# The low half of every weight chunk is split off when the next chunk's split begins

## The chip, the cores and the metric

The kernel runs on one core of a Trainium2 chip. The metric is the device time of one execution in microseconds; the median of several runs of the kernel before is 2160.03 us.

## The reference, cut to what matters

Two transformer blocks are computed in float32 on 512 tokens of width 1024. The first is an S5 state-space mixer beside a sliding-window attention, then a gated FFN; the second is a dilated-window attention, an FFN, an HGRN2 mixer, and an FFN. The bulk is products of a 512 x 1024 activation with weights:

```python
proj = hn @ w_in[l]                                   # mix
h = h + rms_norm(merged @ w_out[l], g_post_mix[l])
gu = hn @ w_gate_up[l]                                # ffn1
ff = (jax.nn.silu(gu[..., :D_FF]) * gu[..., D_FF:]) @ w_down[l]
...
proj = (x @ w_in).reshape(B, S, N_GROUPS, 3, ATTN_HEADS, ATTN_HEAD_DIM)   # attn
return jnp.square(jax.nn.relu(x @ w_up)) @ w_down                         # ffn2_0, ffn2_1
q_raw, f_raw, i_raw = jnp.split(x @ w_in, [H * K, 2 * H * K], axis=-1)    # hgrn
```

## The kernel before, in words

The stages run one after the other: mix, ffn1, attn, ffn2_0, hgrn, ffn2_1. The activations stay in SBUF. All weights are packed beforehand in the order of their use into 328 chunks of 128 x 1024 float32 values, and the class `Stream` feeds them to every stage.

A product in float32 is made of three TensorE passes on reduced-precision operands: each operand is split into a high part, `hi`, and a low part, `lo = value - hi`, and hi·hi, hi·lo and lo·hi are added in PSUM. For weights this split is done in `Stream._split`: SP starts the DMA of a chunk into one of three `wst` buffers (L170), ScalarE (ACT) copies it rounded into `whi` (L183), and VectorE (DVE) subtracts to get `wlo` (L184). There are 6 buffers (`SLOTS`) of `whi` and `wlo`. For activations the split is at L312 and L313 (`xh` on ACT, `xl` on DVE), for the hidden values of the FFN at L469 and L470 (`hh`, `hl`).

Each engine executes its instructions in the order in which the program issues them. `take` hands out the chunks that are used next and first calls `prefetch`, which splits up to `ahead` = 4 chunks further on, at most 5 past the oldest chunk of the same `take`; `more` does the same in the middle of a product. `_split(i)` also starts loads up to chunk i + 2, and such a load has to wait until its `wst` buffer was read by the `hi` and the `lo` of three chunks ago.

In an FFN stage `up` takes one chunk for each 128 rows of hidden values (24 matmuls of 512 columns, L260 to L262), applies the activation function (`hid`: `r`, `h`, `hh`, `hl`, L464 to L470 in ffn2), and `down` takes four chunks at once for the product with w_down (96 matmuls, L370 to L372). `banks` (L357 to L385) sets the order of those 96. A stage begins with `up_first`, which takes four chunks and computes their first 256 columns while the layer norm of the last tokens (L343 to L355: `nm`, `x` L350, `x` L352) is still under way. In mix, the first chunk (u0) is split before everything else by `prefetch(0, 0)`.

Of the kernel before, what the change touches and what calls it, by code (L numbers as in the profile page):

```python
# [26 lines left out]
F32 = mybir.dt.float32  # L27
# [128 lines left out]
class Stream:  # L156
# [3 lines left out]

    def __init__(self, K, labels, dram):
        self.K, self.labels, self.dram = K, labels, dram
        self.loaded, self.split, self.used = 0, 0, 0
        self.st, self.hl = {}, {}

    def _load(self):
        i = self.loaded
        if i < len(self.labels):
            t = self.K.wst.tile([128, CE], F32, name="wst")
            self.K.nc.sync.dma_start(t, self.dram[i])  # L170
            self.st[i] = t
        self.loaded += 1

    def _split(self):
        i = self.split
        K = self.K
        while self.loaded <= i + self.STAGE_AHEAD:
            self._load()
        if i < len(self.labels):
            t = self.st.pop(i)  # L180
            hi = K.wsp.tile([128, CE], FR, name="whi")
            lo = K.wsp.tile([128, CE], FR, name="wlo")
            K.nc.scalar.activation(hi, t, AF.Copy)  # L183
            K.nc.vector.tensor_sub(lo, t, hi.bitcast(F32))  # L184
            self.hl[i] = (hi, lo)
        self.split += 1

    def prefetch(self, upto, oldest):

        while self.split <= min(upto, oldest + self.SLOTS - 1):  # L190
            self._split()
# [5 lines left out]
    def take(self, *labels, ahead=AHEAD):  # L197

        i0, out = self.used, []
        for label in labels:  # L200
            i = self.used
            assert self.labels[i] == label, (self.labels[i], label)
            self.prefetch(i + ahead, i0)
            self.used += 1
            out.append(self.hl.pop(i))
        return out

# [1645 lines left out]
```

## Time and profile before

| what | value |
|---|---|
| median of 3 runs | 2160.03 us (2159.95 to 2162.28) |
| profiled execution | 2164.82 us, its span 2163.0 us |
| mean granted clock of TensorE | 0.982 |
| busy share PE / PEld / DVE / ACT / POOL | 96% / 81% / 56% / 37% / 12% |
| all waits of PE for other engines, added up | about 62 us |
| DVE at `wlo` L184, busy | 436.3 us in 328 instructions |
| ACT at `whi` L183, busy | 331.7 us in 328 instructions |
| weight chunk, from issue of its DMA to landing | 3.8 us (median) |
| spacing of matmuls, read from the timelines | 0.23 us (512 columns), 0.12 us (256 columns), 0.21 us (256 columns at the lower clock) |

PE is TensorE's matmuls and PEld its weight loads, which run beside the matmul before. What PE waits for decides the time; idle time of the other engines costs nothing by itself. In the rows further down, a bracket as [0.33 <-DVE wlo L184] says how long the engine was idle before the row and who released it. Of consecutive DVE rows the next one starts some 0.07 us before the recorded end of the one before.

### The profile page before, as it was taken

Reading aid. Unit: us, or ns where it says so; the run is one execution under the profiler, and the core shown is the slowest. Engines: PE = TensorE matmul, PEld = TensorE weight load, DVE = VectorE, ACT = ScalarE, POOL = GpSimd, SP = SyncE. Lnnn points to the kernel's source line nnn. Section 1 sums busy time; section 2 is a strip of 40 time slices with the busy share of each in tenths; the row PEclk is TensorE's granted clock in tenths of the full one; section 3 lists DMA queues with packets and bytes.
Section 4 is the critical chain, followed back from the end, with each engine's and each line's share of the span. In section 5 each row is a group of like instructions: output and inputs, shape, how many; then the busy total and the mean of one; then the engine's idle time right before and its main releaser. Section 6 shows DMA issues by size and latency. Waiting matters only on the chain.

```text
span 2163.0 us, 30385 instructions
## 1 busy us (share of the span) xinstructions
PE 2083.6 (96%) x12196; PEld 1759.6 (81%) x12196; DVE 1217.7 (56%) x2129; ACT 793.1 (37%) x1470; POOL 269.7 (12%) x325
## 2 busy tenths in 40 slices
PE   6888999999999999999998999999999999999997
PEld 5876788888888888888887888888888878888885
DVE  6876453334366666667766644444565566444444
ACT  5346343222233444443344432223254434222331
POOL 3740100000003212121220100000100001000001
PEclk9979999999999999999999999999999999999998
DMA  3201232223225333333333222232232222222221
GB/s 128 79 23 40 108 117 98 98 78 117 98 68 188 116 113 118 108 98 109 107 115 130 87 89 98 78 108 97 91 106 69 79 78 88 100 85 97 100 96 69
DMA packets 75662, 209.35 MB, mean 97 GB/s; under 512 B 21248, under 2 KB 26016, under 8 KB 75520
## 3 DMA queue, kind: packets, MB, share of 16 engines
q1 hardware_dynamic: 66560, 181.13, 25.0%
q0 software_dynamic: 6816, 19.83, 3.2%
q10 hardware_dynamic: 2144, 6.45, 0.9%
q8 instruction: 96, 1.57, 0.3%
q14 instruction: 46, 0.38, 0.1%
HBM read 186.29 MB, written 4.29 MB: 88 GB/s over the span
## 4 chain that ended last, share of the span: by engine, by line
PE 57%; issue 24%; DVE 3%; POOL 1%; ACT 1%; DMA 1%; POOLq 0%; ACTq 0%; DVEq 0%
PE mm L260 13%; PE mm L261 13%; PE mm L262 13%; PE dn L371 4%; PE dn L370 4%; PE dn L372 4%; PE o L741 1%; PE dn L669 1%; DVE P L648 1%; DVE wlo L184 1%; POOL rv L306 1%; POOL rr L308 1%; PE dn L720 1%; PE dn L718 0%; DMA wst<-in_wstream 0%
## 5 line engine op out<-in xcount | busy, mean ns | idle before, releaser
L260 PE MATMUL mm<-xh,whi 128*128 128x512 f32 (+1 forms) x1488 | 562.7, 378 | 8.4 <-ACT whi L183 5.3
L261 PE MATMUL mm<-xl,whi 128*128 128x512 f32 (+1 forms) x1488 | 558.1, 375 | 2.7 <-DVE xl L313 2.7
L262 PE MATMUL mm<-xh,wlo 128*128 128x512 f32 (+1 forms) x1488 | 557.5, 375 | 0.5 <-DVE wlo L184 0.5
L184 DVE TENSOR_TENSOR wlo<-wst,whi 128x1024 fp32r<-128x1024 f32 x328 | 436.3, 1363 | 167.0 <-ACT whi L183 165.9
L183 ACT ACTIVATE whi<-wst 128x1024 fp32r<-128x1024 f32 x328 | 331.7, 1050 | 353.6 <-PE dn L371 222.0
L260 PEld LDWEIGHTS mm<-xh,whi 128*128 128x128 f32 x1488 | 282.8, 190 | 63.0 <-ACT whi L183 5.6
L261 PEld LDWEIGHTS mm<-xl,whi 128*128 128x128 f32 x1488 | 282.9, 190 | 52.3 <-DVE xl L313 3.8
L262 PEld LDWEIGHTS mm<-xh,wlo 128*128 128x128 f32 x1488 | 282.8, 190 | 51.5 <-DVE wlo L184 0.8
L371 PE MATMUL dn<-whi,hl 128*128 128x512 f32 x688 | 271.5, 395 | 0.0
L370 PE MATMUL dn<-whi,hh 128*128 128x512 f32 x688 | 271.0, 394 | 0.1
L372 PE MATMUL dn<-wlo,hh 128*128 128x512 f32 x688 | 268.5, 390 | 0.0
L260 PE MATMUL mm<-whi,xh 128*128 128x256 f32 x608 | 177.3, 292 | 1.9 <-DVE kT L1197 1.9
L261 PE MATMUL mm<-wlo,xh 128*128 128x256 f32 x608 | 173.3, 285 | 0.0
L262 PE MATMUL mm<-whi,xl 128*128 128x256 f32 x608 | 173.1, 285 | 0.0
L480 DVE SCALAR_TENSOR_TENSOR x<-x,dn 128x512 f32<-128x512 f32 x112 | 75.6, 685 | 169.1 <-PE dn L372 169.1
L306 POOL TENSOR_SCALAR rv<-ss 128x1 f32<-128x1 f32 (+1 forms) x42 | 26.3, 626 | 1041.9 <-ACT junk L348 443.2
L370 PEld LDWEIGHTS dn<-whi,hh 128*128 128x128 f32 x688 | 129.4, 188 | 30.4 <-DVE x L341 0.5
L372 PEld LDWEIGHTS dn<-wlo,hh 128*128 128x128 f32 x688 | 129.3, 188 | 29.3
L371 PEld LDWEIGHTS dn<-whi,hl 128*128 128x128 f32 x688 | 129.5, 188 | 26.7
L260 PEld LDWEIGHTS mm<-whi,xh 128*128 128x128 f32 x608 | 117.8, 194 | 7.3 <-issue 4.6
L261 PEld LDWEIGHTS mm<-wlo,xh 128*128 128x128 f32 x608 | 117.9, 194 | 0.2
L262 PEld LDWEIGHTS mm<-whi,xl 128*128 128x128 f32 x608 | 117.8, 194 | 0.0
(385 smaller groups left out, 2542.9 us busy)
## 6 DMA issues: line engine op xcount, KB each, us to landing
wst<-in_wstream SPq DMA_DIRECT2D x328, 512.0 KB, 3.8
qks<-qkT POOLq DMA_DIRECT2D x96, 128.0 KB, 2.8
v<-gb SPq DMA_DIRECT2D x128, 32.0 KB, 1.8
X<-in_x SPq DMA_DIRECT2D x4, 512.0 KB, 7.7
xn<-in_x POOLq DMA_DIRECT2D x4, 512.0 KB, 4.5
x_d<-x POOLq DMA_DIRECT2D x4, 512.0 KB, 6.7
x<-x_d POOLq DMA_DIRECT2D x4, 512.0 KB, 6.9
out<-x SPq DMA_DIRECT2D x4, 512.0 KB, 2.6
```

The source lines that it names most:

```text
L183: K.nc.scalar.activation(hi, t, AF.Copy)
L184: K.nc.vector.tensor_sub(lo, t, hi.bitcast(F32))
L260: mm(ps, wh, xh, start=first, stop=False, skip_group_check=True)
L261: mm(ps, wh, xl, start=False, stop=False, skip_group_check=True)
L262: mm(ps, wl, xh, start=False, stop=last, skip_group_check=True)
L306: self.nc.gpsimd.tensor_scalar(v[:, :n], ss, scale, eps, op0=OP.mult, op1=OP.add)
L308: self.nc.gpsimd.tensor_tensor(r[:, :n], v[:, :n], self.nhalf[:, :n], op=OP.pow)
L370: mm(p, hT[i][0][:, c], w[i][0][:, n], start=i == 0, stop=False)
L371: mm(p, hT[i][1][:, c], w[i][0][:, n], start=False, stop=False)
L372: mm(p, hT[i][0][:, c], w[i][1][:, n], start=False, stop=i == m - 1)
L480: nc.vector.scalar_tensor_tensor(x, x, ALPHA if first else 1.0, ps, op0=OP.mult, op1=OP.add)
L648: nc.vector.tensor_scalar(s, s, E[:, g, u, h:h + 1], None, op0=OP.mult)
```

## The change

`_split` no longer issues the subtraction directly behind the copy. It notes it in `self.due`, and `low` issues it either when the next chunk's split begins or when `take` hands out the chunk itself.

```diff
@@ __init__
         self.st, self.hl = {}, {}
+        self.due = None
...
     def _split(self):
         i = self.split
         K = self.K
+        self.low()
         while self.loaded <= i + self.STAGE_AHEAD:
             self._load()
...
             K.nc.scalar.activation(hi, t, AF.Copy)
-            K.nc.vector.tensor_sub(lo, t, hi.bitcast(F32))
             self.hl[i] = (hi, lo)
+            self.due = i, lo, t, hi
         self.split += 1
+
+    def low(self, upto=None):
+
+        if self.due and (upto is None or self.due[0] <= upto):
+            _, lo, t, hi = self.due
+            self.due = None
+            self.K.nc.vector.tensor_sub(lo, t, hi.bitcast(F32))
...
             self.prefetch(i + ahead, i0)
             self.used += 1
+            self.low(i)
             out.append(self.hl.pop(i))
```

The order of instructions on PE, ACT, POOL and SP is the same in both kernels; on DVE only the `wlo` rows move. In the rows of the changed kernel line numbers are 10 or 11 higher (L184 is L195, L470 is L480, L352 is L362).

On DVE, in ffn2_0, this is the stretch around the first `down` of the stage. `h` and `hl` belong to the hidden values of four `up` chunks, the `wlo` rows are chunks of this `down` and, in the row marked x2 or x3, also of the next `up`, and the x rows add the output of `down`. Before:

```order
L184 TENSOR_TENSOR wlo<-wst,whi 128x1024
L466 TENSOR_TENSOR h<-r 128x512
L470 TENSOR_TENSOR hl<-h,hh 128x512
L184 TENSOR_TENSOR wlo<-wst,whi 128x1024
L466 TENSOR_TENSOR h<-r 128x512
L470 TENSOR_TENSOR hl<-h,hh 128x512
L184 TENSOR_TENSOR wlo<-wst,whi 128x1024 x2
L480 SCALAR_TENSOR_TENSOR x<-x,dn 128x512 x8
```

In the changed kernel:

```order
L195 TENSOR_TENSOR wlo<-wst,whi 128x1024
L476 TENSOR_TENSOR h<-r 128x512
L480 TENSOR_TENSOR hl<-h,hh 128x512
L195 TENSOR_TENSOR wlo<-wst,whi 128x1024
L476 TENSOR_TENSOR h<-r 128x512
L480 TENSOR_TENSOR hl<-h,hh 128x512
L195 TENSOR_TENSOR wlo<-wst,whi 128x1024 x2
L490 SCALAR_TENSOR_TENSOR x<-x,dn 128x512 x8
```

The single `wlo` ahead of the last `h` and `hl` was the fourth chunk of the `down`; now it is the third, and the fourth is the first of the two behind `hl`.

On DVE, at the start of ffn2_0, `nm`, `x` and `x` are the layer norm of the last 128 tokens and `xl` is the split of the transposed activations. Before:

```order
L184 TENSOR_TENSOR wlo<-wst,whi 128x1024
L345 TENSOR_SCALAR nm<-sums_ln_mix_g_10315 128x1
L350 SCALAR_TENSOR_TENSOR x<-x,nm,gb 128x1024
L352 SCALAR_TENSOR_TENSOR x<-x,rr,gb 128x1024
L184 TENSOR_TENSOR wlo<-wst,whi 128x1024
L313 TENSOR_TENSOR xl<-dn,xh 128x4x128 x4
```

In the changed kernel:

```order
L195 TENSOR_TENSOR wlo<-wst,whi 128x1024
L355 TENSOR_SCALAR nm<-sums_ln_mix_g_10314 128x1
L360 SCALAR_TENSOR_TENSOR x<-x,nm,gb 128x1024
L362 SCALAR_TENSOR_TENSOR x<-x,rr,gb 128x1024
L195 TENSOR_TENSOR wlo<-wst,whi 128x1024 x2
L323 TENSOR_TENSOR xl<-dn,xh 128x4x128 x4
```

The `wlo` of the third chunk of ffn2_0 stood ahead of `nm`; now it stands behind the second `x`, in front of the fourth chunk's.

On DVE, at the start of mix, the X rows scale the input, and `fr` and `fi` are the last of some forty small instructions that prepare the rotation angles. Before:

```order
L892 SCALAR_TENSOR_TENSOR X<-X,rr,gb 128x1024 x2
L184 TENSOR_TENSOR wlo<-wst,whi 128x1024
L313 TENSOR_TENSOR xl<-dn,xh 128x4x128 x2
L892 SCALAR_TENSOR_TENSOR X<-X,rr,gb 128x1024
...
L960 TENSOR_TENSOR fr<-t_0_185,t_1_186 128x16
L961 TENSOR_TENSOR fi<-t_3_188,t_1_186 128x16
L184 TENSOR_TENSOR wlo<-wst,whi 128x1024 x2
L313 TENSOR_TENSOR xl<-dn,xh 128x4x128 x4
```

In the changed kernel:

```order
L902 SCALAR_TENSOR_TENSOR X<-X,rr,gb 128x1024 x2
L323 TENSOR_TENSOR xl<-dn,xh 128x4x128 x2
L902 SCALAR_TENSOR_TENSOR X<-X,rr,gb 128x1024
L323 TENSOR_TENSOR xl<-dn,xh 128x4x128 x2
...
L970 TENSOR_TENSOR fr<-t_0_184,t_1_185 128x16
L971 TENSOR_TENSOR fi<-t_3_187,t_1_185 128x16
L195 TENSOR_TENSOR wlo<-wst,whi 128x1024 x3
L323 TENSOR_TENSOR xl<-dn,xh 128x4x128 x4
```

The first chunk's `wlo` stood third, ahead of the first `xl`; now it is the first of three behind the angles.

## Rows read from the trace of the kernel before

**Rows 1.** The page, part 1: busy us (share of the span) xinstructions of each engine.

```profile
PE 2083.6 (96%) x12196; PEld 1759.6 (81%) x12196; DVE 1217.7 (56%) x2129; ACT 793.1 (37%) x1470; POOL 269.7 (12%) x325
```

**Rows 2.** Waits of the whole span: engine, line, releaser: us in total, times, longest.

```profile
DVE wlo L184 <- ACT whi L183: 165.9, 128, 20.2
```

**Rows 3.** Waits of the DMA-issuing queue of SP, with the same columns.

```profile
SPq L170 <- DVE wlo L184: 1600.2, 283, 77.2
```

**Rows 4.** Line 184: durations (min/median/max ns), first and last start, forms.

```profile
L184 DVE TENSOR_TENSOR wlo<-wst,whi x328: 1209/1221/4197, 11.4 to 2127.5; 128x1024 fp32r<-128x1024 f32 x164
```

**Rows 5.** Timeline near 1772 us: start us, duration us, engine, line, [idle before <-releaser].

```profile
1771.78 0.39 PE L371 MATMUL dn<-whi,ol 128*128 128x512 f32 x1
...
1772.07 0.19 PEld L372 LDWEIGHTS dn<-wlo,oh 128*128 128x128 f32 x1 [0.33 <-DVE wlo L184]
...
1772.40 0.39 PE L370 MATMUL dn<-whi,oh 128*128 128x512 f32 x1
```

**Rows 6.** Timeline of ffn2_0 around its first change from up to down products.

```profile
1290.47 1.23 DVE L184 TENSOR_TENSOR wlo<-wst,whi 128x1024 fp32r<-128x1024 f32 x1 [0.26 <-ACT whi L183]
...
1295.11 0.69 DVE L470 TENSOR_TENSOR hl<-h,hh 128x512 fp32r<-128x512 f32 x1 [0.70 <-ACT hh L469]
...
1296.51 0.19 PEld L372 LDWEIGHTS dn<-wlo,hh 128*128 128x128 f32 x1
```

**Rows 7.** Timeline of the start of mix (0 to 92 us).

```profile
16.25 0.42 PE L262 MATMUL mm<-xh,wlo 128*128 128x256 f32 x1
...
26.84 0.17 DVE L961 TENSOR_TENSOR fi<-t,t 128x16 f32<-128x16 f32 x1
...
27.16 0.58 PE L260 MATMUL mm<-xh,whi 128*128 128x256 f32 x1 [5.32 <-ACT whi L183]
...
32.22 1.04 PE L325 MATMUL dn<-ident,X 128*128 128x128 f32 x8
...
45.40 1.23 DVE L184 TENSOR_TENSOR wlo<-wst,whi 128x1024 fp32r<-128x1024 f32 x1 [3.87 <-ACT whi L183]
...
90.86 0.69 PE L1193 MATMUL mm<-ident,qk 128*128 128x128 f32 x2 [4.59 <-ACT v L1221]
```

**Rows 8.** Timeline of mix, first group of products with w_out.

```profile
217.93 0.40 PE L372 MATMUL dn<-wlo,oh 128*128 128x512 f32 x1
...
218.21 0.75 DVE L1353 SCALAR_TENSOR_TENSOR ol<-sig,m_g_so,oh 128x512 fp32r<-128x512 f32 x1 [0.79 <-ACT oh L1352]
```

**Rows 9.** Timeline of the start of ffn2_0.

```profile
1207.88 1.28 DVE L352 SCALAR_TENSOR_TENSOR x<-x,rr,gb 128x1024 f32<-128x1024 f32 x1 [0.71 <-POOL rr L308]
...
1208.03 0.28 PE L262 MATMUL mm<-xh,wlo 128*128 128x256 f32 x1
```

**Rows 10.** Timeline of the start of hgrn.

```profile
1569.85 0.28 PE L262 MATMUL mm<-xh,wlo 128*128 128x256 f32 x1
...
1572.31 1.22 DVE L184 TENSOR_TENSOR wlo<-wst,whi 128x1024 fp32r<-128x1024 f32 x1
```

**Rows 11.** Timeline of the end of ffn1: two down products back to back.

```profile
616.38 0.69 DVE L1723 TENSOR_TENSOR acc<-acc,dn 128x512 f32<-128x512 f32 x1 [2.06 <-PE dn L372]
...
617.10 0.19 PEld L372 LDWEIGHTS dn<-wlo,hh 128*128 128x128 f32 x1
```

**Rows 12.** Timeline of the end of attn.

```profile
1138.86 0.39 PE L372 MATMUL mm<-wlo,xh 128*128 128x512 f32 x1
...
1140.58 1.90 DVE L776 TENSOR_TENSOR xl<-x,xh 128x512 fp32r<-128x512 f32 x3 [2.45 <-ACT xh L775]
...
1146.01 1.35 PE L669 MATMUL dn<-qkT 64*128 64x128 f32 x7 [4.31 <-DVE ML L637]
```

**Rows 13.** Timeline of the start of ffn1.

```profile
272.89 0.39 PE L260 MATMUL mm<-xh,whi 128*128 128x256 f32 x1 [3.03 <-ACT xh L312]
```

**Rows 14.** Windows: each engine's busy us (instructions), granted TensorE clock, DMA share, GB/s.

```profile
272.80:276.00 3.20, 2.77 (x12) 2.58 (x13) 2.99 (x4) 2.50 (x5) 1.53 (x4) 0.56 0.41 154
...
1146.00:1150.00 4.00, 3.99 (x20) 3.48 (x21) 3.93 (x32) 3.46 (x16) 0.00 (x0) 0.50 0.98 382
```

## The prediction

> **What bounds the kernel now.** I read the busy times first: PE is busy for 96% of the span, DVE for 56% [rows 1]. So the time changes only where PE waits more or less. The table of waits comes next. Before its `wlo`, DVE stands 128 times for the ACT copy that feeds it, 165.9 us in all, and everything behind it on DVE stands too [rows 2]. This is what the change can shorten: the subtraction is issued when its input has long been there. But DVE is not the bound; all that PE waits for, on any engine, is about 62 us in the table ahead. So I went to the timelines and asked of each of the 328 chunks: when does PEld first want its `wlo`, and what stands on DVE in front of it now. What is saved is mostly idle time on an idle engine; what is paid is every place where `wlo` now comes after PEld wants it.
>
> **The change part by part.** Nothing is added or removed: 328 subtractions of 1.22 us (median) stay [rows 4], and PE, ACT, POOL and SP keep their order. What moves is each `wlo` on DVE, past what stands between its own split and the next one.
>
> *The price of a late `wlo`* is in the trace: a weight load waited 0.33 us. The matmul two rows on would have come at 1771.78 + 2 x 0.23 = 1772.24 and came at 1772.40, 0.16 late [rows 5]. A weight load runs ahead of its matmul, so the delay is the lateness less some 0.17 us, and nothing below that.
>
> *Up to down in ffn2.* The fourth `down` chunk's `wlo` ran at 1290.47, far ahead of its use. Now it stands behind `h` and `hl` of the last `up` chunk. `hl` runs from 1295.11 to 1295.80, so `wlo` runs from about 1295.73 to 1296.95, and PEld wants it at 1296.51 [rows 6], with 0.05 us for the signal 0.49 late, which costs 0.32. There are 7 such changes in each of ffn2_0 and ffn2_1: 14 x 0.32 = 4.5 us, between 0 (if `hl` comes half a microsecond earlier) and 14 x 0.49 = 6.9. In ffn1 the same reading leaves 0.2 us to spare; I take nothing.
>
> *Starts of a stage.* The third chunk's `wlo` now stands behind the last norm. In ffn2_0 `x` L352 starts at 1207.88 and takes 1.28; `wlo` would end at 1207.88 + 1.20 + 1.22 = 1210.30. The matmul that needs it came at 1208.03 [rows 9]: 2.25 us late. In hgrn six small instructions are in front as well: `wlo` would start at 1572.31 where another one did before, end at 1573.53, and was needed at 1569.85 [rows 10], 3.7 us. The starts of ffn1 and ffn2_1 read the same way give 2.6 and 2.55. The four together: 11.1 us.
>
> *Two `down` products back to back.* At the end of ffn1 the last chunk's `wlo` now waits for the last addition. That starts at 616.38 and takes 0.69, so `wlo` ends near 616.99 + 1.22 = 618.21, and PEld wants it at 617.10 [rows 11]: 1.1 late, about 1.0 of delay. The ends of ffn2_0 and ffn2_1 repeat it, the last chunks of w_out in hgrn give about 1.2, the first product of attn about 0.65. Together 5.0.
>
> *Mix, w_out.* `wlo` now follows `ol`, which starts at 218.21 and takes 0.75: 218.89 to 220.11. Its matmul came at 217.93 [rows 8]. That is 2.2 at most. DVE no longer stands for the copy earlier in the group, which may bring `ol` up to 1 us forward: 1.2 to 2.2, I take 1.7.
>
> *End of attn.* `wlo` of the fourth chunk of w_out follows three `xl`, 1140.58 to 1142.48, and ends near 1143.65. Its matmul came at 1138.86 [rows 12]: about 4.8 us. But 4.31 us of waiting follow at 1146.01, for the softmax behind the same DVE work. After the stall come 6 matmuls (1.4 us at full pace, 2.7 at half), about 0.9 us of scores and three softmax rows of 0.35: 1147.2 to 1148.5. So PE goes on 1.2 to 2.5 us later than at 1146.01; I take 2.0.
>
> *Start of mix.* The first `wlo` moves past 41 instructions behind the angles (L961 at 26.84). The matmul that needs it came at 16.25 and now comes at about 28.3. The 22 that follow it, some at half pace, take some 4.1 us, transposes 0.8, the next 24 matmuls 24 x 0.12 = 2.9: the transposes that stood at 32.22 come at about 36.1, +3.9. Before, PE idled here anyhow: 5.32 us until 27.16. DVE then stood 3.87 us for a copy at 45.40 [rows 7] and about 2.9 a little later; these end, so DVE is some 3 us ahead where it hands its tables to POOL, and the wait of 4.59 at 90.86 [rows 7] shrinks by that. With 0.5 us for a later small exposure the start of mix is worth -1.5, between -4 and +4.
>
> *What is given back elsewhere.* DVE is free earlier in the tails of the stages. From mix to ffn1 2.1 us of standing for a copy go, and I take 2.25 off PE's waits there, of which the largest is the 3.03 at 272.89 [rows 13]. In the same way hgrn's tail gives 1.25, the other stage ends 1.85, softmax in attn 1.0: -6.3, between -2 and -12.
>
> The sum: 4.5 + 11.1 + 5.0 + 1.7 + 2.0 - 1.5 - 6.3 = +16.5. Some of the 11.1 falls where PE would have waited for the same norm shortly after; I take 1.5 off for it and say **+15**. The profiled execution then goes from 2164.82 to about 2180; it is 4.8 above the median of the runs, which goes from 2160.03 to about **2175**. A measurement of this kernel tells about 0.2% (4.3 us) from no change.
>
> **The clock.** After the wait of 3.03 at 272.89 the granted clock was 0.56 over the next 3.2 us, after the 4.31 at 1146.01 it was 0.50 over 4 us [rows 12 to 14]: near half pace, the lower of the two levels, a loss of some 1.5 to 2 us each. After the 0.33 at 1772.07 matmuls kept 0.23 [rows 5]. So the small stalls cost no more than themselves. Those of 2.25 to 3.7 us at the starts of stages lie near the one that lowered the clock.
>
> The Trainium skill, "TensorE: Matmul & The Clock Gate", section "Why this matters for your kernels", warns that a gap between bursts of matmuls brings the clock back to the lower level, which the two waits above bear out. [...]
>
> **The rivals.** *Larger, some +20 to +25* (chance 0.18). The four starts lose the clock, 4 x 1.75 = +7, on top of 15: 2182. For it speaks [rows 13, 14]; against it that the stalls split a burst instead of following a longer gap. A mechanism in the same direction: SP's loads stand for `wlo` 283 times [rows 3], and each `wst` buffer now comes free one split later; where several splits are bunched the copy could wait for its DMA. Against it: a load lands in 3.8 us and the `up` chunks are used every 5.6.
>
> *No measurable change* (chance 0.12). The starts of stages cost half, 5.5, because norms come earlier with a freer DVE, the start of mix gives 4, the tails 9: 4.5 + 5.5 + 5 + 1.7 + 2 - 4 - 9 = +6, and a small miss elsewhere brings it within 4.3. That needs nearly every bound at its good end.
>
> *Faster* (chance 0.05). One mechanism: in mix, PE waits for DVE and ACT in the chain of tables, scans and rotations, among them the 5.32 and 4.59 of [rows 7]. If DVE's standing behind the copies is what delays that chain, mix gives back much more than 1.5. It decides from 15 + 4.3 + 1.5 = 21 us in mix; the 5.32 can't go, since its copy stands on ACT, and the 4.59 with its loss of clock is worth 6.5. So this is unlikely.
>
> **How the numbers follow.** My forecast, +8 to +20, has 0.65; the larger case 0.18, no change 0.12, faster 0.05. Slower is the first two, 0.83. The range leaves out about one in ten on each side: from +4 (2164) to +24 (2184).
>
> **What the profile of the changed kernel would show.** PE and PEld in `down` wait for `wlo` 14 times by some 0.3 to 0.5 us in ffn2; single waits of 2 to 4 us for `wlo` stand at the starts of ffn1, ffn2_0, hgrn and ffn2_1, about 1 us at three ends of stages, 12 us near 28 us. DVE's 165.9 us of waits for `whi` shrink to a small part. ACT and POOL keep their busy times. The prediction is wrong if PE's waits for `wlo` add up to less than 15 us beside the one at 28, or if PE's waits for other work in mix and the tails shrink by more than 10.

## The result, and the profile after

The changed kernel took 2182.02 us (median of 4 runs, 2179.74 to 2184.02), the kernel before 2160.77 on the same chip. The ratio is 1.0097, with a 95% interval of 1.0082 to 1.0111: 18 to 24 us slower. The prediction said 2175 (2164 to 2184).

The page of the changed kernel, parts 1 and 5, answers to [rows 1]. No engine has noticeably more to do, DVE even less, and yet the span is longer.

```profile
span 2178.0 us, 30330 instructions
...
PE 2082.9 (96%) x12196; PEld 1754.6 (81%) x12196; DVE 1186.1 (54%) x2129; ACT 794.4 (36%) x1470; POOL 267.5 (12%) x325
...
L195 DVE TENSOR_TENSOR wlo<-wst,whi 128x1024 fp32r<-128x1024 f32 x328 | 400.6, 1251 | 110.4 <-ACT whi L185 109.6
```

This is what line 195, the moved subtraction, does now: durations, what DVE idled for in front of it, and who waited for it (us, times).

```profile
L195 DVE TENSOR_TENSOR wlo<-wst,whi x328: 1210/1220/2325, 26.9 to 2142.6; 128x1024 fp32r<-128x1024 f32 x164
...
  ACT whi L185: 109.6, 33
...
  PEld mm L272: 22.7, 8
  PE mm L272: 21.0, 8
  PEld dn L382: 16.8, 22
  PE dn L382: 6.3, 5
  PEld mm L382: 5.1, 1
  PEld mm L271: 5.0, 3
  PE mm L382: 4.7, 1
  PE mm L271: 4.4, 3
```

Both halves of the exchange are here. DVE stood for the copy 33 times instead of 128, but still for 109.6 us of the 165.9 [rows 2]: two thirds of its standing stayed. The longest subtraction fell from 4197 ns [rows 4] to 2325, and all of them together from 436.3 us of work to 400.6. In return PEld, which had waited for `wlo` in hardly any place, waits 34 times and 49.6 us in all. PE's own waits for `wlo` went from 0.5 us to 36.4, all its other waits together from 62.2 to 40.8. The net is 14.5 us, close to the 14.9 us by which the two profiled executions differ.

With both kernels' matmuls laid side by side in program order (PE's order is the same), the difference of the two start times, the lateness, shows where time goes. Five rows of the changed kernel, in the order of the program: two at the start of mix, then a group of w_out, the end of attn and the start of hgrn.

```profile
28.19 0.58 PE L272 MATMUL mm<-xh,wlo 128*128 128x256 f32 x1 [11.76 <-DVE wlo L195]
...
89.83 0.44 PE L1203 MATMUL mm<-ident,qk 128*128 128x128 f32 x2 [0.25 <-ACT v L1231]
...
219.46 0.49 PE L382 MATMUL dn<-wlo,oh 128*128 128x512 f32 x1 [3.13 <-DVE wlo L195]
...
1143.20 0.79 PE L382 MATMUL mm<-wlo,xh 128*128 128x512 f32 x1 [4.68 <-DVE wlo L195]
...
1577.78 0.39 PE L272 MATMUL mm<-xh,wlo 128*128 128x256 f32 x1 [3.04 <-DVE wlo L195]
```

The first matmul of mix that needs a low part came at 16.25 [rows 7] and comes at 28.19. By the row at 89.83, which was at 90.86 with a wait of 4.59 [rows 7], PE is 1.0 us ahead of before: the chain on POOL that it waits for started earlier. At 219.46 it falls 1.5 behind (217.93 in [rows 8]). It is 4.0 behind at the start of attn, gets back to about 0 by its end, and from ffn2_0 on it loses: 3.6 us behind at the start of ffn2_0, 7.9 at the start of hgrn (1569.85 in [rows 10]), 15.1 at the last product. In ffn2 the stall looks like this (DVE, DVE, PEld), to be held against [rows 6]:

```profile
1298.11 0.69 DVE L480 TENSOR_TENSOR hl<-h,hh 128x512 fp32r<-128x512 f32 x1 [0.70 <-ACT hh L479]
...
1298.71 2.35 DVE L195 TENSOR_TENSOR wlo<-wst,whi 128x1024 fp32r<-128x1024 f32 x2
...
1299.98 0.19 PEld L382 LDWEIGHTS dn<-wlo,hh 128*128 128x128 f32 x1 [0.47 <-DVE wlo L195]
```

The two profiled executions differ by 14.9 us (2164.82 and 2179.74), the medians by 21. The profiled execution of before is on the slow side of its runs, the one of after on the fast side of its own; sizes in time below are therefore from the timed runs, and places from the traces.

### The profile page after: what moved, and what is told of

The parts are those of the page before. It is cut to its first block, busy times and chain, and to the rows that moved or that the text cites. A ratio compares the mean times of both kernels' runs of the same rounds, so it can differ in the third digit from the quotient of the medians.

```text
span 2178.0 us, 30330 instructions
## 1 busy us (share of the span) xinstructions
PE 2082.9 (96%) x12196; PEld 1754.6 (81%) x12196; DVE 1186.1 (54%) x2129; ACT 794.4 (36%) x1470; POOL 267.5 (12%) x325
## 3 DMA queue, kind: packets, MB, share of 16 engines
q1 hardware_dynamic: 66560, 181.13, 24.6%
## 5 line engine op out<-in xcount | busy, mean ns | idle before, releaser
L195 DVE TENSOR_TENSOR wlo<-wst,whi 128x1024 fp32r<-128x1024 f32 x328 | 400.6, 1251 | 110.4 <-ACT whi L185 109.6
L476 DVE TENSOR_TENSOR h<-r 128x512 f32<-128x512 f32 x64 | 44.3, 692 | 133.5 <-ACT r L474 133.5
```

Of the source, the lines that this page charges most:

```text
L195: self.K.nc.vector.tensor_sub(lo, t, hi.bitcast(F32))
L476: nc.vector.tensor_mul(h, r, r)
```

## The experiments

All ten kernels split the 328 chunks into those that are deferred as in the change and those whose low part is issued directly behind the copy, as before. Each time is compared with the kernel before, run beside it (medians 2162.04 to 2162.18 us). The edit is two lines in the changed kernel's `_split`, with a set of chunk numbers:

```diff
             self.due = i, lo, t, hi
+            if i not in LATE:
+                self.low()
```

**Only what was waited for is kept early.** All chunks are deferred but 31 of the 34 that PEld waited for; before the change it already waited for the other three.

```diff
+NOW = {0, 9, 17, 24, 85, 89, 163, 169, 170, 179, 187, 195, 203, 211, 219, 227, 229, 233, 234, 237, 261, 265, 266, 275, 283, 291, 299, 307, 315, 323, 325}
...
             self.due = i, lo, t, hi
+            if i in NOW:
+                self.low()
```

> The changed kernel, but for 31 chunks whose low part was waited for in its trace (the first, single ones in mix, attn and hgrn, the second and third at the starts of stages, the last before a product that follows another directly, and the fourth of 14 products in ffn2) the subtraction is issued directly behind the copy again; the other 297 stay deferred. Theory (late low parts cost, a freer DVE gives back): the costs go and the gains stay, by the two traces some 5 us at the start of mix, 3 in the tail of mix, 4 in the softmax of attn, 2 in other tails: 2146 to 2154 us, against 2160.8 before. Rival (deferral itself is harmful, since each load is freed later): within 3 us of before, or slower than it.

2151.49 us, ratio 0.9953 (0.9940 to 0.9965): 8 to 13 us faster than before. Deferral as such does no harm; its price lies in those 31 of 328 chunks. This run also settles what the prediction feared of the loads. ACT's copies do wait longer for their DMA when everything is deferred, but they do so here as well, in a version that is faster than before. These are the waits of before, of the change and of this run, in us, times and longest:

```profile
ACT whi L183 <- DMA wst<-in_wstream: 47.1, 14, 6.5
...
ACT whi L185 <- DMA wst<-in_wstream: 134.5, 35, 6.9
...
ACT whi L188 <- DMA wst<-in_wstream: 135.9, 35, 6.8
```

**The fourth chunk of 14 `down` products.**

```diff
+LATE = {179, 187, 195, 203, 211, 219, 227, 275, 283, 291, 299, 307, 315, 323}
```

> The kernel before with one part of the change: only the fourth chunk of 14 products with w_down in ffn2_0 and ffn2_1 is deferred behind h and hl. Theory (a late low part costs its lateness less what the weight load is ahead): 14 x 0.3 to 0.4 us, +4 to +5.5 us. Rival 1 (hidden): within 1.5 us of before. Rival 2 (every small stall also lowers the clock): over +15 us.

2166.71 us, ratio 1.0022 (1.0012 to 1.0031): +4.8 us (2.6 to 6.7). In its timeline, one of the stalls, and the matmul after it:

```profile
1845.79 0.19 PEld L387 LDWEIGHTS dn<-wlo,hh 128*128 128x128 f32 x1 [0.54 <-DVE wlo L200]
...
1846.13 0.39 PE L385 MATMUL dn<-whi,hh 128*128 128x512 f32 x1
```

A load 0.54 late costs about 0.4, and the matmul spacing behind it stays as before: the granted clock over the next 4 us is 1.00.

**Starts of stages.**

```diff
+LATE = {24, 170, 234, 266}
```

> The kernel before with one part of the change: only the third chunk of ffn1, ffn2_0, hgrn and ffn2_1 is deferred, behind the norm of the last tokens. Theory: four stalls of 1.5 to 3.3 us and some of the clock behind them, +8 to +13 us. Rival (the stalls stand in for waits on the same norm shortly after): less than +4 us.

2167.99 us, ratio 1.0034 (1.0022 to 1.0046): +7.4 us (4.8 to 9.9), just under the +8 to +13 of the theory. Laid beside before, the four chunks lose 0.6, 1.5, 2.8 and 1.7 us at their stalls; in the whole change the same four lose 1.7, 2.2, 3.3 and 2.2. The difference is on DVE. Alone, moving the third chunk's subtraction lets the norm in front of it start about 1 us sooner; in the whole change the second chunk's subtraction has moved into the gap. The rival is out: no wait shortly behind the stalls of ffn1, ffn2_0 and ffn2_1 takes their loss back, and behind hgrn's it is 0.9 us.

**The first chunk.**

```diff
+LATE = {0}
```

> The kernel before with one part of the change: only the very first chunk's low part is deferred, behind the angles. Theory (the early stall is paid, and only the other deferrals in mix win it back): TensorE about 4 us late at 45 us and still some 3 to 4 us late at 91 us, +3 to +5 us. Rival (the idle time that was there before and the chain of tables on GpSimd take it up by themselves): within 1 us of before.

2165.63 us, ratio 1.0018 (1.0009 to 1.0026): +3.9 us (1.9 to 5.6). Its DVE still stands for the two next copies (first two rows). PE, 5.1 us late at the transposes of 32.22, still waits for the same `v` behind POOL's chain, 5.3 us later than at 90.86 in [rows 7]:

```profile
50.55 1.23 DVE L200 TENSOR_TENSOR wlo<-wst,whi 128x1024 fp32r<-128x1024 f32 x1 [3.90 <-ACT whi L188]
56.64 1.23 DVE L200 TENSOR_TENSOR wlo<-wst,whi 128x1024 fp32r<-128x1024 f32 x1 [2.87 <-ACT whi L188]
...
96.11 0.69 PE L1208 MATMUL mm<-ident,qk 128*128 128x128 f32 x2 [4.68 <-ACT v L1236]
```

So the early idle time takes up only a part of the late first chunk; the other deferrals in mix do the rest.

**Mix and attn alone.** Deferred are mix, the first chunks of ffn1 (22 to 33) and attn up to number 159, without five that were waited for.

```diff
+LATE = (set(range(34)) | set(range(88, 160))) - {0, 9, 17, 24, 89}
```

> The kernel before with a part of the change: low parts are deferred in mix and in attn up to its last scores alone, without the first chunk and four others that were waited for; ffn1, ffn2_0, hgrn, ffn2_1 and the end of attn keep the order of before. Theory (what a freer DVE gives back lies in mix and attn): as fast as the kernel that kept the 31 needed chunks, or 1 to 3 us faster, since that one lost some 2 us at the start of ffn2_0: 2147 to 2152 us. Rival (FFN and hgrn give back too): 2153 us or more.

2150.25 us, ratio 0.9947 (0.9933 to 0.9960): -11.5 us (-14.5 to -8.7), level with the first experiment. Within the noise, all that a freer DVE gives lies in these two stages. The row that stood at 90.86 with 4.59 of waiting [rows 7] shows the part of mix:

```profile
87.19 0.44 PE L1208 MATMUL mm<-ident,qk 128*128 128x128 f32 x2 [1.29 <-ACT v L1236]
```

**Attn alone.**

```diff
+LATE = set(range(90, 160))
```

> The kernel before with a part of the change: low parts are deferred in attn alone, up to its last scores. Theory (in attn the softmax comes earlier by about 1.1 us in each of four heads' rounds, because the subtraction no longer stands on DVE for its copy and for GpSimd's rotary products): -3.5 to -6 us. Rival (the gain is in mix alone): within 2 us of before.

2159.22 us, ratio 0.9989 (0.9980 to 0.9998): -2.4 us (-4.3 to -0.4), less than expected, since the fourth round lost 0.7 us. The first three gain 1.1 each, the softmax before them being earlier. In attn the trace of before shows what the deferral avoids, early in the stage (DVE, POOL):

```profile
666.85 4.81 DVE L184 TENSOR_TENSOR wlo<-wst,whi 128x1024 fp32r<-128x1024 f32 x2 [3.58 <-ACT whi L183]
...
668.16 2.41 POOL L592 TENSOR_TENSOR qka<-qkT,rot 128x1024 f32<-128x1024 f32 x1
```

and in the trace of after, where such a pair runs clear of POOL's product:

```profile
665.09 2.44 DVE L195 TENSOR_TENSOR wlo<-wst,whi 128x1024 fp32r<-128x1024 f32 x2 [0.65 <-ACT whi L185]
```

Thirteen subtractions of before take 3.7 to 4.2 us, all of them in attn; in the changed kernel none takes more than 2.33. So in attn the change saves more than standing: the subtractions themselves are no longer stretched.

**Nine single chunks.**

```diff
+LATE = {9, 17, 85, 89, 163, 229, 237, 261, 325}
```

> The kernel before with a part of the change: only nine single chunks are deferred that were waited for outside the 14 products of ffn2, the starts of stages and the first chunk (two in mix, the last of ffn1, the first product of attn, the fourth of w_out in attn, and five in ffn2_0, hgrn and ffn2_1 at ends of stages). Theory: their stalls of 0.8 to 4.8 us add up to 16 us, of which some 2 come back where a wait follows anyhow: +10 to +16 us. Rival (waits behind them take up most): under +6 us.

2178.34 us, ratio 1.0072 (1.0059 to 1.0085): +15.6 us (12.8 to 18.4). This is the largest part of the change, and the one that the prediction undersized most. At the end of attn the fourth chunk of w_out stalls PE for 4.7 us; most of it comes back at the next softmax, where before PE waited 4.31 [rows 12], and 1.6 go again behind it. From one side to the other the lateness grows by 2.0.

**One of them, and why it is large.** It is the last chunk of the first group of w_out in mix.

```diff
+LATE = {17}
```

> The kernel before with a part of the change: only the last chunk of the first group of w_out in mix is deferred. Theory (the subtraction now runs beside GpSimd's sum of squares and takes 2.3 us instead of 1.2, and the stall brings the clock down): a stall of about 3 us and +3 to +5 us in all. Rival (as predicted, the subtraction takes 1.22 us): a stall of 1.2 to 2.2 us and +1 to +2.2 us.

2166.45 us, ratio 1.0019 (1.0010 to 1.0027): +4.1 us (2.2 to 5.8). The rows are DVE's and POOL's:

```profile
210.45 1.34 POOL L1374 TENSOR_TENSOR sq<-sq,s 128x512 f32<-128x512 f32 x1 [6.02 <-ACT s L1373]
...
210.55 1.78 DVE L1410 TENSOR_TENSOR yg<-qT,m_g_ao 128x512 f32<-128x512 f32 x1
...
213.64 0.68 DVE L1410 TENSOR_TENSOR yg<-qT,m_g_ao 128x512 f32<-128x512 f32 x1
...
217.74 1.32 POOL L1374 TENSOR_TENSOR sq<-sq,s 128x512 f32<-128x512 f32 x1 [5.95 <-ACT s L1373]
217.84 3.43 DVE L200 TENSOR_TENSOR wlo<-wst,whi 128x1024 fp32r<-128x1024 f32 x2
...
220.19 0.50 PE L387 MATMUL dn<-wlo,oh 128*128 128x512 f32 x1 [2.01 <-DVE wlo L200]
```

The same instruction, `yg`, takes 1.78 us beside POOL's addition and 0.68 without it. The deferred subtraction is the first of the pair at 217.84; PE goes on at 220.19, so it ran for 2.3 us, not 1.22. The matmul comes 2.3 us late. Over the four microseconds from 223 the granted clock (the third number from the end of the row) is 0.50, where before it was 0.75 over 220 to 224. So the lower clock was there in part without the stall, and the stall makes it last longer:

```profile
223.00:227.00 4.00, 4.00 (x41) 3.40 (x38) 0.16 (x1) 0.73 (x2) 1.24 (x2) 0.50 0.97 358
```

Laid beside before, the lateness grows there from 2.3 to 4.0 us.

**The same without POOL's addition.** `LATE = {17}`, and:

```diff
                 A.activation(s1, y, AF.Square)
-                G.tensor_add(sq, sq, s1)
```

> The kernel with only the last chunk of the first group of w_out deferred, and with GpSimd's addition of the squares (L1359 of before) left out, so that three quarters of the sum of squares behind one of the norms are missing. Theory (GpSimd's addition beside it is what stretches that subtraction from 1.2 to 2.3 us): the subtraction takes 1.22 us and the stall falls from 2.3 to about 1.2 us, +1.5 to +3.5 us in all. Rival (something else, as the DMA traffic, stretches it): still 2.3 us and the same stall.

2162.17 us, ratio 1.0006 (0.9997 to 1.0014): no longer told from before.

```profile
215.44 2.35 DVE L200 TENSOR_TENSOR wlo<-wst,whi 128x1024 fp32r<-128x1024 f32 x2
...
216.71 0.50 PE L387 MATMUL dn<-wlo,oh 128*128 128x512 f32 x1 [0.29 <-DVE wlo L200]
```

The subtraction takes 1.2 us again, while the DMA engines moved about as much beside it (265 GB/s, 274 in the run above), so the rival is out. The stall, now 0.29 us, fell further than expected, because `yg` ahead of it lost 1.1 us as well; with no addition to wait for, other things in the group came earlier too, so the time by itself doesn't size the addition's share.

**A version that beats both.** Deferred are mix, the first two chunks of ffn1, and attn from its third chunk up to the third of w_out, without three in mix:

```diff
+LATE = (set(range(24)) | set(range(90, 163))) - {0, 9, 17}
```

> The kernel before with the low parts deferred in mix up to the last chunk of its own and in attn up to the third chunk of w_out, without the first chunk and two in mix that were waited for. Theory (the gain lies in mix and attn, and the variant that ended two chunks earlier in attn lost its fourth round of softmax by this): 0 to 2 us faster than that one, 2147 to 2151 us. Rival (the end of attn loses again): 2152 us or more.

2149.30 us, ratio 0.9943 (0.9930 to 0.9957): 12 us faster than before, 33 us faster than the change. Its fourth round of attn gains 1.1 us in the trace, but its time is not told apart from that of the version that defers up to 159.

## Why the prediction was right, point by point

The direction, the range and the mechanism held: DVE's standing was idle time except in two stages, and the price was the places where `wlo` came after PEld wanted it. The parts, measured one by one, add up to 4.8 + 7.4 + 3.9 + 15.6 - 11.5 = +20.2 us, against 21.0 (17.7 to 24.0) for the whole. Each part is known to 2 or 3 us only, and the second chunks at three starts are in none of them, so the agreement shows no more than that no large part is missing.

The forecast itself, +15, was 6 us short: the time lies just past the +8 to +20 that had most of the chance, on the 2182 of the larger rival. By the number alone that rival would have won. But its clock loss was seen at one start of four (see below), and moving the four starts alone costs 7.4 us, not 11 and 7 more; what was short is the single chunks.

- *Up to down in ffn2*: 4.5 predicted, 4.8 measured. The lateness of 0.49 was 0.47 to 0.54. My 0.17 us of head start for a weight load was a little too much (0.54 late cost 0.4). In the trace of that run the seven stalls of ffn2_1 lose 2.8 us, and ffn2_0 as a whole loses 1.1, since some of it came back in small steps. Why is not shown.
- *Starts of a stage*: 11.1 less 1.5 predicted, 7.4 alone. In the whole change the four third chunks lose 9.4 us and three second chunks, which I had not counted, 0.5 to 0.7 each: about 11.1. Alone they lose less because DVE's norm is then about 1 us earlier; I had no term for the order in which these moves depend on each other.
- *Start of mix*: 3.9 predicted for the first chunk, +3.9 (1.9 to 5.6) measured. That the figures are equal is luck: mine was for the transposes of 32.22, which came 5.1 late, and the time is what is left of that at the end. What the other deferrals give back there held: the wait of 4.59 became 0.25, where I had it shrink by 3.
- *What is given back*: -6.3, and 5.9 in the -1.5 of the start of mix, -12.2 together; measured -11.5. The sum agrees by luck, for its division was off: attn gives 2.4 or more, not 1.0, and hgrn and the FFN stages nothing that could be measured. I had also taken every subtraction at its median of 1.22; in attn before they were stretched, and a part of the gain there is that they no longer are.
- *Single chunks*: the term that was mis-sized. Ends of stages 5.0, w_out in mix 1.7, end of attn 2.0 and 0.5 for one in mix are 9.2; measured 15.6 (12.8 to 18.4). In the trace of that run, laid beside before, most of them cost what I had: the end of attn 2.0, three ends of stages 1.0 each, w_out in hgrn 1.2, and the first product of attn 0.7, since of the 1.7 it loses 1.0 come back at the next wait. Four places make the difference. The chunk of w_out in mix cost 4.1 in time, since its subtraction met POOL's addition and the lower clock lasted longer; I had taken the median duration of [rows 4] although that row's longest, 4197 ns, said that it can be stretched. The other chunk in mix lost 1.1, not 0.5, its subtraction being stretched to 2.2 us in the same way. One chunk of hgrn (237) I had not listed; it loses 1.25. And at the end of ffn2_0 PE waits 0.94 for a norm that came in time before, behind a copy on ACT that stood 5.64 for its DMA. That the DMA is the reason is not tested.
- *The clock*: the larger rival said that the four starts would lower it. After the change the granted clock behind the stalls of 3.13 (222 to 227 us), 4.68, 1.93 and 3.04 us was as in the first four rows; 1.00 is the level of 2.4 GHz, 0.50 that of 1.2. The last row is about the stretch of the first one, in the kernel before.

```profile
222.00:227.00 5.00, 5.00 (x63) 4.34 (x61) 1.31 (x2) 0.72 (x2) 2.14 (x2) 0.50 0.86 312
1143.20:1147.20 4.00, 4.00 (x13) 2.87 (x15) 2.63 (x10) 1.30 (x5) 1.54 (x3) 0.50 0.73 211
1211.60:1215.60 4.00, 4.00 (x35) 4.00 (x36) 2.39 (x4) 0.78 (x2) 0.00 (x0) 1.00 0.69 215
1577.80:1581.80 4.00, 4.00 (x23) 4.00 (x24) 2.26 (x3) 0.00 (x0) 0.00 (x0) 0.65 0.68 219
...
220.50:225.50 5.00, 5.00 (x36) 4.07 (x33) 1.88 (x3) 1.35 (x3) 1.98 (x4) 0.66 0.97 383
```

Only the one of 3.04, at the start of hgrn, lowered a clock that was at its upper level before. The one of 3.13 made a stretch at the lower level longer (0.50 instead of 0.66). The one of 4.68 at the end of attn shows nothing, because before the clock was at 0.50 there too [rows 14]. The one of 1.93 did not lower it. Of the four starts only hgrn's paid: 1.2 us went to the clock, and 0.9 came back at the next wait. After those of ffn1 and ffn2_1 the granted clock was 1.00 as after ffn2_0's. By the rule of the Trainium skill ("TensorE: Matmul & The Clock Gate", "Why this matters for your kernels") a gap lowers the clock; the trace agrees for hgrn's stall and shows the 1.93 us of ffn2_0 to be harmless. Over the whole span the mean granted clock even rose, from 0.982 in the profiled execution of before to 0.986 in that of after.

- *The signs*: the 14 small waits, the 11.8 us at 28 and the three of 0.8 at ends of stages were there. Three of the four starts waited less than the 2 to 4 us that I gave, 1.4 to 1.9. DVE's waits for `whi` did not shrink to a small part. Of the two signs of being wrong the first stayed away: PE's waits for `wlo` beside the first are 24.6 us, more than 15. The second appeared: PE's waits for other work shrank in mix alone from 47.0 to 33.9 us, by more than 10. Of these 13 us 5.3 are the wait at 27.16, whose place the late first `wlo` took, so by this sign a gain could not be told from a wait that only changed its name.
- *No change* and *faster* fell. The mechanism of the faster rival was real: of the 11.5 us given back mix has the larger part. But that is far from the 21 that it needed, and it shows its sign only once the late chunks are taken out.

## What to carry to other kernels

Ask of a moved instruction not how much idle time its engine gets back, but at each place when its first reader wants it and what now stands ahead of it; here 31 places in 328 decided. Where a deferral pays in some stages and costs in others, choose per stage: the same edit is worth -12 us when it is kept to mix and attn without the chunks that were waited for there, and +21 us everywhere. And look up with what a moved instruction will then run side by side, for its duration may not be the median's.

## What the runs showed of the hardware

In these runs a DVE operation on two SBUF operands took far longer while GpSimd (POOL) worked on SBUF: `yg` 1.78 instead of 0.68 us, the subtraction 2.3 instead of 1.22, and 4.81 instead of 2.44 for a pair beside a 2.41 us product on GpSimd. The Trainium skill, "SBUF — State Buffer", section "Who interferes with whom", says that a DVE instruction with two SBUF inputs and a GpSimd instruction that reads SBUF contend, and calls the pair of ports that they share an exclusive lock. The trace agrees: `yg` took 1.1 us longer where 1.24 us of the addition were still to run, and the pair 2.4 us longer, about the whole product. Leaving the addition out brought `yg` and the subtraction back to 0.68 and 1.2.
